# A decoder layer's input projection: 22 column blocks taken in pairs, ahead of the head groups, and the scan's y products two chunks at a time

## The chip, the core and the metric

The kernel runs on one core of a Trainium2 chip. The metric is device time in microseconds of one execution. A core has a matrix engine (TensorE, PE in the profile; its weight loads are shown as PEld), a vector engine (VectorE, DVE), a scalar engine (ScalarE, ACT), GpSimd (POOL), and SyncE (SP), which issues nearly all DMAs of this kernel.

## What is computed

One step of a hybrid decoder layer on 1024 prompt tokens and 8 decode tokens, T = 1032 token columns in all, model width 1024.

```python
xn = rms_norm(x, p['norm_mix_pre'])
z, xbc, dt_raw, u_pool, gate_a, gate_b = split(xn @ p['w_in'])   # 2048 | 4096 | 32 | 1024 | 1024 | 1024
xbc_c = silu(causal_conv(xbc, conv_w, conv_b))                    # x (2048), B (8 x 128), C (8 x 128)
y = ssd_scan(xs, dt, a, B, C, h0) + d_skip * xs                   # 8 groups of 4 heads, chunks of 128 tokens
y_a = rms_norm(y * silu(z), ssm_norm)
y_b = pool_mix(u_pool, ...)                                       # trailing means of 2/4/8/16, grouped product
merged = sigmoid(gate_a) * (y_a @ w_branch_a) + sigmoid(gate_b) * (y_b @ w_branch_b)
h = x + rms_norm(merged @ w_out)
out = h + rms_norm((silu(g) * up) @ w_ffn_out)                    # g, up = rms_norm(h) @ w_ffn_in
```

## The kernel before

Everything is held transposed: 128 features on the partitions, the 1032 tokens along the free dimension. A product in fp32 precision is made of three matmuls of a shorter type (`mm3`, L230 to L232): the weights are split in a high and a low part (`wh`, `wl`, made by a copy on ACT, L166, and a subtraction, L167), the activations too (`xh`, `xl`), and high·high, high·low and low·high are summed in PSUM.

The input projection's columns come in blocks of 128: 16 of z (`WZ`), 16 of x, 8 of B, 8 of C, 8 of the pooling input (`WU`), 8 and 8 of the two gates (`WGA`, `WGB`). A block takes three units (`in_unit`), one for each third of the tokens (344 columns); a unit is 8 feature rows times 3 matmuls, 24 matmuls into one PSUM bank of the tag `pj`, which has 4 banks. The other four banks are `T` (2), `S` (1) and `y` (1).

The order of the stages:

1. Norm, the time steps dt and the pooling branch: per pooling group two blocks are projected (`pool_proj`), averaged on DVE (`pool_group`), split, and multiplied by a small matrix (`pool_mix`). The last group's product is made inside the first head group.
2. Head groups 0 to 7. `group_proj(g)` makes the six blocks of group g (B, C, x0, x1, z0, z1: 18 units). Each of the first four is followed by a convolution: ACT L593, three DVE instructions L595, ACT L596, DVE L597. Each z unit ends in a tanh on ACT (L610) and a DVE instruction (L611). `ssd(g-1)`, the scan of the group before, is interleaved, one step of it after each unit (`interleave(..., 1)`). A scan has 18 steps: in an even step `stage1(c)` of chunk c, in an odd one `stage2` of the chunk three steps earlier, and decode work on some.
3. `gates`: the 16 gate blocks, with `ssd(7)` interleaved, one step after each unit; the gates are stored in memory (`s_ga`, `s_gb`).
4. Branch products (`quarters`, six of them), merge, output projection, norms, FFN and final norm. FFN in (around L1094) already uses seven products of 258 columns where the plain form has eight.

In a scan, `stage1(c)` transposes B and x of the chunk into a `T` bank (L667 to L670), makes `xdt`, `wx` and `CB` on DVE (L675, L677, L679), loads the decay rows into a tile `E` of three buffers by DMA (L681), and turns them into the chunk's 128x512 decay matrix (ACT L683, L685, DVE L686). `stage2(c)` makes the state update and the old state's part in the `S` bank (L703, L705), then eight matmuls of 64 columns of the array into the `y` bank (L709): two chunks share that one bank, half each, and after the odd chunk DVE reads it (L724). DVE also reads `S` (L716, L719), POOL scales the state (L715) and adds to Y (L728).

The program is written in this order, and a scheduler lays out each engine's queue from it before the run: the order in the text is a priority, and an instruction that the scheduler holds to be ready may go ahead of an earlier one that it holds not to be. On the chip each queue is then worked off strictly in order, the queue of SP's DMAs too. Row buffers (`row`, 36 of them with 128x1032 or a little more) are shared by nearly everything.

Of the kernel before, what the change touches and what calls it, by code (L numbers as in the profile page):

```python
# [16 lines left out]
P = 128  # L17
# [6 lines left out]
G = 8  # L24
# [29 lines left out]

PP_G1, PP_GPOST, PP_GFFN, PP_GFPOST = 0, 8, 16, 24
# [16 lines left out]
def interleave(main, side, every):  # L72
    n = 0
    for _ in main:
        n += 1
        if side is not None and n % every == 0:
            if next(side, StopIteration) is StopIteration:
                side = None
    if side is not None:
        for _ in side:  # L80
            pass
# [3 lines left out]
def layer_kernel(ctx: ExitStack, tc: tile.TileContext, xT, wi, wdt, wpool, wba, wbb, wo, wfi,  # L85
# [9 lines left out]
    ps = ctx.enter_context(tc.tile_pool(name="ps", bufs=2, space=PSUM))  # L95
# [3 lines left out]

    def bank(tag):  # L100
        return ps.tile([P, 512], F32, name=tag, tag=tag, bufs={"pj": 4, "T": 2, "S": 1, "y": 1}[tag])

# [1 line left out]
    plan = []  # L104

# [3 lines left out]
    def plan_weights():  # L109
        def u_blocks(gi):  # L110
            for kb in range(2):
                want(("in", WU + 2 * gi + kb), wi[WU + 2 * gi + kb], eng=pool if 2 * gi + kb == 1 else dve)
        u_blocks(0)
        for gi in range(3):
            u_blocks(gi + 1)
            want(("pool", gi), wpool[gi], 512)
        for g in range(G):
            for i, blk in enumerate((WB + g, WC + g, WX + 2 * g, WX + 2 * g + 1, WZ + 2 * g, WZ + 2 * g + 1)):
                want(("in", blk), wi[blk])
                if g == 0 and i == 2:  # L120
                    want(("pool", 3), wpool[3], 512)
        for base in (WGA, WGB):
            for ob in range(KT):
                want(("in", base + ob), wi[base + ob])
        for qi in range(6):
            for obp in range(4):
                want(("br", qi, obp), wba[qi, obp] if qi < 4 else wbb[qi - 4, obp], eng=pool if qi == 0 else dve)
# [16 lines left out]
    def w_dma():  # L144
        i = stage["nd"]
        if i < len(plan):
            _, src, n, _, _, kind = plan[i]
            if kind == "big":
                raw = big(n, "wu")
            else:  # L150
# [40 lines left out]
    x_rows = [row(name="xrow") for _ in range(KT)]  # L191
# [36 lines left out]

    def mm3(out, wh, wl, xh, xl, start, stop):
        pe.matmul(out, wh, xh, start=start, stop=False)  # L230
        pe.matmul(out, wh, xl, start=False, stop=False)  # L231
        return pe.matmul(out, wl, xh, start=False, stop=stop)  # L232

# [131 lines left out]
    def pool_group(gi, us):  # L365
        w = 2 << gi
        ds = []
        for kb in range(2):
# [12 lines left out]
            while st < w:  # L381
# [6 lines left out]
                st *= 2  # L388
            ss = const.tile([P, NS], F32, name="ss", tag="ss", bufs=2)
# [7 lines left out]
            ds.append(d)  # L397
        return ds
# [12 lines left out]
    def pool_mix(gi, dh, dl):  # L411
        wh, wl = load_w("pool", gi)
        for ob in range(2):
            blk = 2 * gi + ob
            yb = row(name="yb")
            for th in range(3):
                pt = bank("pj")
# [109 lines left out]

    dt_setup()
    us = pool_proj(0, True)
    pend = pool_split(pool_group(0, us))  # L530
    an = dt_phase(dt_mm(2))
    us = pool_proj(1)
    pool_mix(0, *pend)
    pend = pool_split(pool_group(1, us))
    dt_phase2(an)
    us = pool_proj(2)
    pool_mix(1, *pend)
    pend = pool_split(pool_group(2, us))
    us = pool_proj(3)
    pool_mix(2, *pend)  # L540
    last_mix = pool_group(3, us)

# [1 line left out]
    s_y = dram.tile([16, P, T], F32, name="s_y")  # L544
    s_ga = dram.tile([KT, P, T], F32, name="s_ga")
    s_gb = dram.tile([KT, P, T], F32, name="s_gb")
# [17 lines left out]
    def conv_proj(g):  # L564
# [4 lines left out]
        for j, (key, blk, cb) in enumerate((("B", WB + g, 16 + g), ("C", WC + g, 24 + g),  # L569
# [4 lines left out]
            us = U[:, SOFF:SOFF + 32].rearrange("p (b k) -> p b k", k=4)  # L574
# [14 lines left out]

            def tap(k):  # L590
                i = 32 + cb * 4 + k
                return hcw[:, i:i + 1]
            act.activation(out=S[:, :CW], in_=U[:, 0:CW], func=AF.Identity, scale=tap(0), bias=hcw[:, cb:cb + 1])  # L593
            for k in range(1, 4):
                dve.scalar_tensor_tensor(out=S[:, :CW], in0=U[:, k:k + CW], scalar=tap(k), in1=S[:, :CW], op0=ALU.mult, op1=ALU.add)  # L595
            act.activation(out=U[:, 0:CW], in_=S[:, :CW], func=AF.Tanh)  # L596
            dve.scalar_tensor_tensor(out=S[:, :CW], in0=U[:, 0:CW], scalar=1.0, in1=S[:, :CW], op0=ALU.add, op1=ALU.mult)  # L597
# [4 lines left out]
    def z_proj(g):  # L602
        d = grp[g]
        for j in range(2):
            wt = load_in(WZ + 2 * g + j)
            Z = row(name="Z")
            d[f"z{j}"] = Z
            for th in range(3):
                pt = in_unit(wt, th)
                act.activation(out=Z[:, TH[th]], in_=pt, func=AF.Tanh, scale=0.5)  # L610
                dve.scalar_tensor_tensor(out=Z[:, TH[th]], in0=Z[:, TH[th]], scalar=1.0, in1=pt,  # L611
                                         op0=ALU.add, op1=ALU.mult)
                yield
# [4 lines left out]

    def gates():
        n = 0  # L620
        for base, dst in ((WGA, s_ga), (WGB, s_gb)):
            for ob in range(KT):
# [686 lines left out]
```

## Time and profile before

| | |
|---|---|
| Median of three runs | 2149.07 us (2146.68 to 2152.36) |
| Profiled execution, span | 2146.5 us, 2.6 us under the median |
| PE busy | 2091.0 us, 97% of the span |
| PEld busy | 2055.9 us, 96% |
| DVE busy | 1361.0 us, 63% |
| ACT busy | 791.1 us, 37% |
| POOL busy | 406.9 us, 19% |
| Memory traffic | 243.74 MB, 114 GB/s |
| Pooling branch, norm and dt | 0 to about 145 us |
| Group 0's blocks, no scan beside them | about 145 to 222 us |
| Seven groups with a scan beside them | about 222 to 833 us |
| Gates with the last scan | about 833 to 1032 us |
| Branch products | about 1032 to 1306 us |
| Output projection, norms, FFN | the rest |

Matmuls are pipelined, so their shown durations overlap; what one costs in a full stream is the length of the stretch divided by their number. The times at which stages change were read from the first and last start of each line's instructions.

### The profile page before, as it was taken

To read this page: it belongs to the slowest core of one execution; us is meant where nothing else is said; L and a number is where in the kernel's file an instruction comes from. 1 tells how busy PE (TensorE), PEld (TensorE's weight loads), DVE (VectorE), ACT (ScalarE), POOL (GpSimd) and SP (SyncE) were. 2 spreads that over 40 slices of the span, in tenths; PEclk is the share of its full clock that TensorE was granted. 3 is DMA by queue.
4 is the path that set the end of the run, shared out by engine and by line. 5 is a ranking of instruction groups with operands and counts; after the bars stand their busy time and mean duration, and the time that the engine had idled before them with its cause. 6 is when DMAs were issued, how large, how long until landed. Compare 5 with 4: busy or idle time off the path is not lost.

```text
span 2146.5 us, 36509 instructions
## 1 busy us (share of the span) xinstructions
PE 2091.0 (97%) x14722; PEld 2055.9 (96%) x14722; DVE 1361.0 (63%) x2283; ACT 791.1 (37%) x1530; POOL 406.9 (19%) x407
## 2 busy tenths in 40 slices
PE   6999999999999999999999999989999999999997
PEld 5999999999999999999999999989999999999997
DVE  7665578677787776422155775679777666654436
ACT  5443344444444444233331024445333233351112
POOL 3100234424434243210100001352000000000004
PEclk9999999999999999999999999989999999999998
DMA  3332343334434334433343444234322222252133
GB/s 126 97 112 72 100 125 125 124 105 142 139 99 127 116 128 149 137 118 136 117 150 101 145 135 151 101 101 142 96 95 90 72 78 90 99 188 69 40 101 107
DMA packets 121961, 243.74 MB, mean 114 GB/s; under 512 B 24896, under 2 KB 62912, under 8 KB 121792
## 3 DMA queue, kind: packets, MB, share of 16 engines
q1 hardware_dynamic: 121360, 241.12, 35.0%
q8 instruction: 116, 1.90, 0.4%
q14 instruction: 53, 0.43, 0.1%
q10 hardware_dynamic: 432, 0.28, 0.0%
HBM read 189.38 MB, written 51.98 MB: 112 GB/s over the span
## 4 chain that ended last, share of the span: by engine, by line
PE 71%; DVE 8%; ACT 2%; DMA 2%; issue 2%; POOL 2%; SPq 0%; DVEq 0%; ACTq 0%; POOLq 0%
PE pj L230 20%; PE pj L232 20%; PE pj L231 20%; DVE S L595 2%; DMA E<-s_ac 1%; PE y L709 1%; PE y L230 1%; PE y L231 1%; PE y L232 1%; DVE S L597 1%; PE T L230 1%; PE T L232 1%; PE T L231 1%; PE S L231 1%; PE S L232 1%
## 5 line engine op out<-in xcount | busy, mean ns | idle before, releaser
L230 PE MATMUL pj<-xh,wh 128*128 128x344 f32 x1728 | 563.3, 327 | 2.4 <-ACT xh L299 2.4
L231 PE MATMUL pj<-xl,wh 128*128 128x344 f32 x1728 | 553.0, 320 | 0.1
L232 PE MATMUL pj<-xh,wl 128*128 128x344 f32 x1728 | 552.8, 320 | 0.0
L230 PEld LDWEIGHTS pj<-xh,wh 128*128 128x128 f32 x1728 | 324.9, 188 | 14.3 <-issue 11.0
L231 PEld LDWEIGHTS pj<-xl,wh 128*128 128x128 f32 x1728 | 325.5, 188 | 1.4 <-DVE xl L300 0.8
L232 PEld LDWEIGHTS pj<-xh,wl 128*128 128x128 f32 x1728 | 325.2, 188 | 0.0
L167 DVE TENSOR_TENSOR wl<-wr,wh 128x1024 fp32r<-128x1024 f32 (+1 forms) x125 | 170.4, 1364 | 210.0 <-ACT wh L166 210.0
L166 ACT CAST wh<-wr 128x1024 fp32r<-128x1024 f32 x142 | 146.6, 1033 | 363.4 <-PE pj L231 335.5
L917 POOL TENSOR_TENSOR ssacc<-ssacc,sq 128x258 f32<-128x258 f32 (+3 forms) x41 | 43.7, 1072 | 923.8 <-ACT sq L916 917.7
L230 PE MATMUL pj<-qh,wh 128*128 128x344 f32 (+1 forms) x608 | 189.7, 312 | 0.0
L231 PE MATMUL pj<-ql,wh 128*128 128x344 f32 (+1 forms) x608 | 189.7, 312 | 0.0
L232 PE MATMUL pj<-qh,wl 128*128 128x344 f32 (+1 forms) x608 | 189.6, 312 | 0.0
L231 PE MATMUL pj<-al,wh 128*128 128x344 f32 (+2 forms) x528 | 168.9, 320 | 0.0
L232 PE MATMUL pj<-ah,wl 128*128 128x344 f32 (+2 forms) x528 | 168.8, 320 | 0.0
L230 PE MATMUL pj<-ah,wh 128*128 128x344 f32 (+2 forms) x528 | 168.8, 320 | 0.0
L683 ACT ACTIVATE E<-E,acT 128x128 f32<-128x128 f32 x256 | 83.9, 393 | 214.8 <-DMA E<-s_ac 198.1
L595 DVE SCALAR_TENSOR_TENSOR S<-U,hcw,S 128x1056 f32<-128x1056 f32 x96 | 137.3, 1430 | 3.0 <-ACT S L593 2.9
L1172 DVE TENSOR_TENSOR acc<-acc,pj 128x344 f32<-128x344 f32 (+2 forms) x120 | 60.8, 510 | 98.0 <-PE pj L232 97.9
L231 PEld LDWEIGHTS pj<-ql,wh 128*128 128x128 f32 x608 | 114.4, 188 | 0.0
L232 PEld LDWEIGHTS pj<-qh,wl 128*128 128x128 f32 x608 | 114.4, 188 | 0.0
L230 PEld LDWEIGHTS pj<-qh,wh 128*128 128x128 f32 x608 | 114.3, 188 | 0.0
L232 PEld LDWEIGHTS pj<-ah,wl 128*128 128x128 f32 x528 | 99.3, 188 | 0.0
(351 smaller groups left out, 4898.1 us busy)
## 6 DMA issues: line engine op xcount, KB each, us to landing
wr<-wi SPq DMA_DIRECT2D x72, 512.0 KB, 4.3
E<-s_ac SPq DMA_DIRECT2D x64, 256.0 KB, 4.0
wr<-wfi SPq DMA_DIRECT2D x30, 512.0 KB, 3.6
s_act<-wk SPq DMA_DIRECT2D x44, 258.0 KB, 2.0
ar<-s_act SPq DMA_DIRECT2D x22, 516.0 KB, 4.7
wu<-wfi SPq DMA_DIRECT2D x22, 512.0 KB, 3.7
wr<-wfo SPq DMA_DIRECT2D x20, 512.0 KB, 3.7
s_y<-Y SPq DMA_DIRECT2D x16, 516.0 KB, 3.8
```

The lines of the kernel that those rows point to most:

```text
L166: act.copy(out=wh, in_=raw)
L167: eng.tensor_tensor(out=wl, in0=raw, in1=wh, op=ALU.subtract)
L230: pe.matmul(out, wh, xh, start=start, stop=False)
L231: pe.matmul(out, wh, xl, start=False, stop=False)
L232: return pe.matmul(out, wl, xh, start=False, stop=stop)
L595: dve.scalar_tensor_tensor(out=S[:, :CW], in0=U[:, k:k + CW], scalar=tap(k), in1=S[:, :CW], op0=ALU.mult, op1=ALU.add)
L597: dve.scalar_tensor_tensor(out=S[:, :CW], in0=U[:, 0:CW], scalar=1.0, in1=S[:, :CW], op0=ALU.add, op1=ALU.mult)
L683: act.activation(out=E[:, h], in_=E[:, h], func=AF.Relu, scale=-1.0, bias=acT[:, c, 4 * g + h:4 * g + h + 1])
L709: pe.matmul(o, xdt[:, h, :], E[:, h, :], start=True, stop=True)
L917: eng.tensor_tensor(out=sacc[:, sl], in0=sacc[:, sl], in1=q, op=ALU.add)
L1172: dve.tensor_tensor(out=acc[ob][:, sl], in0=acc[ob][:, sl], in1=pt, op=ALU.add)
```

## The change

The core of the diff. What is left out are the tile pools that it opens and closes around the stages (`xp`, `ps1` with three two-bank tiles `dj`, `ps2` with `pj` 3, `T` 2, `S` 1, `y` 2 banks, `ps3` as before), renames, and the same conv code moved into a helper.

```diff
+H = T // 2
+PAIRS = "ga0 ga1 z0 ga2 z1 ga3 gb0 z2 gb1 z3 gb2".split()
+MIXES = {2: 3}
+RING = 3
+PROD1 = ("B11", "T2", "B21", "T3", "T1", "T4", "B22")
...
+    def pair_blocks(name):
...
+        if kind == "z":
+            return WZ + 4 * n + 1, WZ + 4 * n + 3
+        base = (WGA if kind == "ga" else WGB) + 2 * n
+        return base, base + 1
...
+    def t_sums():
+        for k in range(4):
+            a, b, c, d = (x_rows[i][:, sl] for i in (k, 4 + k) for sl in (lo_, hi_))
+            eng.tensor_tensor(out=d, in0=d, in1=b, op=ALU.subtract)
+            eng.tensor_tensor(out=b, in0=b, in1=a, op=ALU.subtract)
+            eng.tensor_tensor(out=a, in0=a, in1=d, op=ALU.add)
+            eng.tensor_tensor(out=c, in0=c, in1=a, op=ALU.subtract)
...
+    def t1_split():
+        for k in range(4):
+            for i, r_ in enumerate((xh[k], xl[k])):
+                sync.dma_start(out=s_b12[i, k], in_=r_[:, hi_].bitcast(F32))
+        for k in range(4):
+            act.copy(out=xh[k][:, hi_], in_=x_rows[k][:, hi_])
+            dve.tensor_tensor(out=xl[k][:, hi_], in0=x_rows[k][:, hi_], in1=xh[k][:, hi_], op=ALU.subtract)
+
+    def restore():
+        for k in range(4):
+            for i, r_ in enumerate((xh[k], xl[k])):
+                sync.dma_start(out=r_[:, hi_].bitcast(F32), in_=s_b12[i, k])
...
+    def prep1(i):
...
+            dve.tensor_tensor(out=s_[:, a_], in0=u_[:, a_], in1=u_[:, b_], op=ALU.add)
+            dve.tensor_tensor(out=s_[:, b_], in0=s_[:, a_], in1=g_[:, a_], op=ALU.subtract)
...
+            dve.tensor_tensor(out=u_[:, a_], in0=g_[:, a_], in1=u_[:, a_], op=ALU.subtract)
...
+            dve.tensor_tensor(out=s_[:, b_], in0=g_[:, b_], in1=s_[:, b_], op=ALU.subtract)
...
+        act.copy(out=w[:, a_], in_=src)
+        dve.tensor_tensor(out=w[:, b_], in0=src, in1=w[:, a_], op=ALU.subtract)
...
+    def product1(i):
...
+        if pi in (0, 1, 3, 4):
+            pair[pi] = dbank()
+        pt = pair[{2: 0, 5: 3, 6: 4}.get(pi, pi)]
...
+        for b_ in range(2):
+            cs = slice(b_ * Q, b_ * Q + Q)
+            o = pt[:, b_ * 512:b_ * 512 + Q]
+            for k in range(4):
...
+                pe.matmul(o, wh_, h[:, cs], start=first and k == 0, stop=False, skip_group_check=True)
+                pe.matmul(o, wh_, l[:, cs], start=False, stop=False, skip_group_check=True)
+                pe.matmul(o, wl_, h[:, cs], start=False, stop=k == 3, skip_group_check=True)
...
+        if pi == 0:
+            act.copy(out=q22, in_=v)
+        elif pi == 1:
+            dve.tensor_tensor(out=q12, in0=q22, in1=v, op=ALU.add)
+        elif pi == 2:
+            act.copy(out=q11, in_=v)
...
+    def finish_pair(name, rs):
...
+        if kind == "z":
+            for j in (1, 0):
+                t = row(name="tz")
+                act.activation(out=t, in_=rs[j], func=AF.Tanh, scale=0.5)
+                dve.scalar_tensor_tensor(out=rs[j], in0=t, scalar=1.0, in1=rs[j], op0=ALU.add, op1=ALU.mult)
+                sync.dma_start(out=s_z[2 * n + j], in_=rs[j])
...
-    last_mix = pool_group(3, us)
+    with tc.issue_after(fence):
+        t_sums()
+    pool_mix(2, *pend1)
+    for i in range(RING):
+        prep1(i)
+    t_split()
...
+    for i, (name, pi) in enumerate(items1):
+        if i + RING < len(items1):
+            prep1(i + RING)
+        product1(i)
...
+        if name != "m" and pi == 6:
+            tails.append(finish_pair(name, pair["rows"]))
...
+    BANKS[0] = {"pj": 3, "T": 2, "S": 1, "y": 2}
+    restore()
...
         def stage2(c, BT, xdt, wx, eA, E):
-            if c % 2 == 0:
-                pend[1] = bank("y")
-            yb = pend[1]
...
-            for h in range(R):
-                o = yv[(h % 2) * 64:(h % 2) * 64 + 64, h // 2, c % 2, :]
-                pe.matmul(o, xdt[:, h, :], E[:, h, :], start=True, stop=True)
+            if c % 2 == 0:
+                pend[0] = xdt, E
+            else:
+                yb = bank("y")
+                for i, (x_, E_) in enumerate((pend[0], (xdt, E))):
+                    for h in range(R):
+                        o = yv[(h % 2) * 64:(h % 2) * 64 + 64, h // 2, i, :]
+                        pe.matmul(o, x_[:, h, :], E_[:, h, :], start=True, stop=True)
...
+            if u == 13:
+                d["z1"] = row(name="Z")
+                sync.dma_start(out=d["z1"], in_=s_z[g])
...
-        interleave(group_proj(g), ssd(g - 1), 1)
-    interleave(gates(), ssd(G - 1), 1)
+        interleave(group_proj(g), ssd(g - 1), 1.17)
+    interleave(gates(), ssd(G - 1), 1.1)
```

After the change:

- Eleven pairs of blocks (four of gate A, three of gate B, and four of z, each the second z block of two groups) are made between the pooling branch and group 0. A pair is a 1024 x 256 weight block times 1032 tokens, cut in two in each dimension; seven products of the halves (sums and differences of weights in `prep1`, of activations in `t_sums` and `t_split`) stand for eight. A product is 2 x 4 x 3 matmuls of 258 columns into a tile of two banks; its result is added to the pair's rows on DVE or copied by ACT. Gates and z then get their tanh and are stored in memory.
- The activation sums T1 take the place of half of four `xh` and `xl` rows, which are stored in memory first (`s_b12`) and loaded again at the end (`restore`).
- The last pooling group's work (`last_pool`) and its product (`m`) lie among the first pairs.
- `group_proj` makes five blocks (15 units); z1 is loaded from memory in the scan's step 13. About 1.17 scan steps go with a unit.
- The scan makes the y products of an even and an odd chunk together, in the odd one's `stage2`, into one of two `y` banks; `xdt` has three buffers, `CB` one. `pj` has three banks in this stage.
- `gates` has only gate B's last two blocks (6 units), then the first branch quarter (24 units of 12 matmuls), with `ssd(7)` at 1.1 steps per unit. The row norm of the scan (`ssm_rms`) moves into the third quarter.

## Rows read from the trace of the kernel before

**Rows 1.** Page, part 1: busy time, share of span and instructions of each engine.

```profile
PE 2091.0 (97%) x14722; PEld 2055.9 (96%) x14722; DVE 1361.0 (63%) x2283; ACT 791.1 (37%) x1530; POOL 406.9 (19%) x407
```

**Rows 2.** Windows: stretch, length, busy us (count) of PE PEld DVE ACT POOL, PEclk, DMA, GB/s.

```profile
200.00:250.00 50.00, 50.00 (x332) 49.03 (x331) 25.63 (x33) 16.20 (x31) 9.93 (x9) 1.00 0.28 94
...
1000.00:1100.00 100.00, 100.00 (x636) 100.00 (x635) 29.38 (x31) 38.31 (x57) 9.61 (x4) 1.00 0.42 148
...
1500.00:1854.00 354.00, 354.00 (x2949) 354.00 (x2950) 256.29 (x496) 118.70 (x242) 0.00 (x0) 1.00 0.27 86
```

**Rows 3.** Instructions of L654, the first of each scan: durations, first and last start.

```profile
L654 PE MATMUL T<-ident,bcs x8: 271/271/272, 221.7 to 833.6; 128*16 128x128 f32 x8
```

**Rows 4.** Waits of all engines: who waited for whom, us, times, longest us.

```profile
PE y L709 <- DVE Y L724: 12.2, 9, 1.6
PE pj L230 <- ACT mo L943: 2.6, 1, 2.6
...
ACT E L683 <- DMA E<-s_ac: 198.1, 39, 9.4
```

**Rows 5.** Timeline of PE, one `stage2` and next scan's start: start, length, merged instructions.

```profile
567.21 0.61 PE L705 MATMUL S<-S,hT 128*128 128x128 f32 x4
567.74 0.66 PE L709 MATMUL y<-E,xdt 128*64 128x128 f32 x8
568.33 0.43 PE L230 MATMUL pj<-xh,wh 128*128 128x344 f32 x1
568.60 0.32 PE L231 MATMUL pj<-xl,wh 128*128 128x344 f32 x1
...
572.21 0.27 PE L654 MATMUL T<-ident,bcs 128*16 128x128 f32 x1
572.32 0.27 PE L667 MATMUL T<-ident,S 128*128 128x128 f32 x1
```

**Rows 6.** Groups by line and form, whole span: count, busy us, mean ns, idle before.

```profile
L1110 DVE TENSOR_TENSOR wk<-wk,pj 128x258 f32<-128x258 f32 x120 | 50.5, 422 | 21.3 <-PE pj L232 20.4
L1129 DVE TENSOR_TENSOR wk<-wk 128x516 f32<-128x516 f32 x40 | 27.8, 696 | 1.7
```

**Rows 7.** Windows of one group's period, columns as in Rows 2.

```profile
514.20:602.00 87.80, 85.63 (x583) 82.20 (x582) 66.64 (x95) 40.81 (x91) 34.25 (x36) 1.00 0.39 124
```

**Rows 8.** DVE's groups by line and form in 539 to 627 us, one group's period.

```profile
L595 DVE SCALAR_TENSOR_TENSOR S<-U,hcw,S 128x1056 f32<-128x1056 f32 x12 | 17.6, 1466 | 0.0
L167 DVE TENSOR_TENSOR wl<-wr,wh 128x1024 fp32r<-128x1024 f32 x6 | 9.6, 1607 | 8.2 <-ACT wh L166 8.2
L686 DVE TENSOR_TENSOR E<-E,CB 128x512 f32<-128x512 f32 x8 | 6.6, 823 | 0.1
L597 DVE SCALAR_TENSOR_TENSOR S<-U,S 128x1056 f32<-128x1056 f32 x4 | 6.2, 1543 | 2.2 <-ACT U L596 2.2
...
L750 DVE TENSOR_TENSOR st<-st,dts 128x1024 f32<-128x1024 f32 x3 | 3.6, 1210 | 0.0
...
L611 DVE SCALAR_TENSOR_TENSOR Z<-Z,pj 128x344 f32<-128x344 f32 x6 | 3.0, 506 | 7.4 <-ACT Z L610 7.4
...
L778 DVE TENSOR_TENSOR Y<-Y,Z 128x1032 f32<-128x1032 f32 x2 | 2.9, 1482 | 0.5 <-POOL Y L728 0.5
...
L754 DVE TENSOR_TENSOR st<-st,bc 128x1024 f32<-128x1024 f32 x1 | 1.2, 1210 | 0.0
```

**Rows 9.** Timeline of DVE and POOL: a weight split beside decode work; x1's last conv step.

```profile
542.67 2.40 POOL L756 TENSOR_TENSOR bc<-st,bc 128x1024 f32<-128x1024 f32 x1 [2.99 <-DVE dx L747]
...
543.26 2.90 DVE L167 TENSOR_TENSOR wl<-wr,wh 128x1024 fp32r<-128x1024 f32 x1
...
553.94 1.26 DVE L597 SCALAR_TENSOR_TENSOR S<-U,S 128x1056 f32<-128x1056 f32 x1 [0.84 <-ACT U L596]
```

**Rows 10.** Tile `qr`, 516 KB loads: time from issue to landing.

```profile
DMA to landing us min/median/max: 4.5/5.6/8.2
```

**Rows 11.** Window at a stall of PE before FFN in, columns as in Rows 2.

```profile
1410.00:1414.00 4.00, 1.27 (x4) 0.97 (x5) 1.28 (x3) 0.81 (x3) 4.00 (x2) 0.50 0.00 0
```

More of the change, by code (lines that the diff above doesn't have):

```diff
@@ L69, in schedule, with interleave @@
         pass
[L72 to L76, printed above, removed]
+def interleave(main, side, steps):
+    for n, _ in enumerate(main):
+        for _ in range(int((n + 1) * steps) - int(n * steps) if side is not None else 0):
             if next(side, StopIteration) is StopIteration:
                 side = None
+                break
     if side is not None:
@@ L188, in load_raw @@
         return raw
-    x_rows = [row(name="xrow") for _ in range(KT)]
+    x_rows = [xp.tile([P, T], F32, name="xrow", tag="x") if k < 4 else row(name="xrow") for k in range(KT)]
     def load_x(th):
@@ L539, in layer_kernel, with last_pool @@
+    fence = last_mm[0].ins
     us = pool_proj(3)
-    pool_mix(2, *pend)
-    last_mix = pool_group(3, us)
+    with tc.issue_after(fence):
+        t_sums()
+    pool_mix(2, *pend1)
+    del pend1
+    for i in range(RING):
+        prep1(i)
+    t_split()
+    x_rows.clear()
+    pend = []
+    ps_ctx.close()
+    ps_ctx = ExitStack()
+    ps[0] = ps_ctx.enter_context(tc.tile_pool(name="ps1", bufs=2, space=PSUM))
+    tails = []
+    def last_pool(us_):
+        ds_ = []
+        yield from pool_steps(3, us_, ds_)
+        dh, dl = [], []
+        for d in ds_:
+            dh.append(row(dt=F32R, name="dh"))
+            act.copy(out=dh[-1], in_=d[:, :T])
+            dl.append(row(dt=F32R, name="dl"))
+            dve.tensor_tensor(out=dl[-1], in0=d[:, :T], in1=dh[-1], op=ALU.subtract)
+            yield
+        pend.append((3, (dh, dl)))
@@ L588, in conv_proj @@
             d[key] = S
[L590 to L597, printed above, removed]
+            conv(U, S, cb)
             if j == 3:
@@ L603, in z_proj @@
         d = grp[g]
[L604 to L613, printed above, removed]
+        wt = load_in(WZ + 2 * g)
+        Z = row(name="Z")
+        d["z0"] = Z
+        for th in range(3):
+            pt = in_unit(wt, th)
+            act.activation(out=Z[:, TH[th]], in_=pt, func=AF.Tanh, scale=0.5)
+            dve.scalar_tensor_tensor(out=Z[:, TH[th]], in0=Z[:, TH[th]], scalar=1.0, in1=pt,
+                                     op0=ALU.add, op1=ALU.mult)
+            yield
     def group_proj(g):
```

303 lines of the change are left out of this document (232 added, 71 removed).

## The prediction

> **What bounds the kernel now.** I read the page's busy times first: PE 97%, its weight loads 96%, DVE 63% [rows 1]. So only what shortens PE's stream, or the few places where PE stands, can pay. Busy time does not price a matmul, since durations overlap; the windows do. Where nothing but 344-column matmuls runs, 636 fit in 100 us: 157.2 ns each. Where nothing but 258-column ones runs (FFN in, itself seven products for eight), 2949 fit in 354 us: 120.0 ns, with DVE busy 72% of that stretch [rows 2]. The second view is the waits: after the start and the norms, PE's largest repeated wait is the y products' for DVE's read of their single bank, 12.2 us in 9 waits [rows 4]. The third is the period of a head group, from the first instruction of each scan: (833.6 - 221.7) / 7 = 87.4 us [rows 3]. In such a period DVE is busy 66.6 us and POOL 34.3 us [rows 7]: far busier than over the whole span, so a shorter period is where a second bound could show.
>
> **Part 1, the pairs.** Removed: 22 blocks of 72 matmuls, so per pair 144 x 157.2 ns = 22.64 us. Added: 7 products of 24 matmuls at 120.0 ns = 20.16 us [rows 2]. Gain 2.48 us a pair, **27.2 us** for eleven. By columns alone it would be an eighth of 22.64, 2.83 us a pair; the narrower matmul carries more overhead, so I take the measured prices. The new DVE work is hidden: per pair 4 weight sums, 7 splits at about 0.70 us (512 columns; the 516-column row is 696 ns), 5 additions from PSUM at 0.70 to 0.84 us (two of 258 columns are 2 x 422 ns [rows 6]; I take 0.75), 11.5 us, and 3 us more for z (two of 1.5): 12 to 15 us in 20, no denser than FFN in's 72%. Two products into the same two-bank tile need the first to be read out in between, but another product of 24 x 0.12 = 2.9 us lies there. If that cover failed, it would cost up to the whole 2.48 us a pair (a rival below).
>
> **Part 2, y products.** The 12.2 us wait arises because the next even chunk reuses the bank before DVE has read it [rows 4]. With two banks the read in question is two chunks older, about 10 us; it is gone, **12.2 us**. What is next late at that place is DVE's read of the `S` bank, needed a chunk later. Merging also drops every other run of 64-column matmuls. Around one such run [rows 5]: the four L705 before it take 0.53 us until it starts, where 128-column matmuls go 0.11 us apart (4 x 0.11 = 0.44), and the first projection matmul after it takes 0.27 instead of 0.157. So entry and exit cost 0.09 + 0.11 = 0.20 us. 32 runs are dropped: at most 6.4 us, nothing if the S products pay the same on leaving. I take **5 us**, since both excesses are seen at this run alone. Sum of gains: 27.2 + 12.2 + 5 = 44.4 us.
>
> **Part 3, three changes of PSUM layout.** New banks wait for the old ones' last reads. The trace has no such change. From below it is 0.4 us (one read, 422 ns [rows 6]), from above a wait of PE for a read by ACT, 2.6 us [rows 4]. I take 1.2 us, nearer to the plain read, each: **3.6 us** (1 to 8).
>
> **Part 4, start of the pairs.** `t_sums` is 16 DVE instructions at 0.70 = 11 us in the last pooling projection, where DVE is about half idle (25.6 of 50 us [rows 2]): hidden. `t_split`, 16 splits, 11 us, falls partly on the first pair, beside 11.5 us of the pair's own work and `last_pool`. T4 is due after five products, 14.4 us; before it lie 12 splits, 8.4 us (t43 and T1), 5.6 us of weight preparation and 3 us of additions: 17 us. Some can be done earlier, but 36 row buffers are nearly all held then (16 `xh`/`xl`, 4 x rows, 12 for T, 4 of the previous mix), so not all. Bounds 0 (done early) and 7 us (the last splits after 14.4 us, with a product's wait); I take **2 us**, the shortfall.
>
> **Part 5, end of the pairs.** `restore` issues 8 loads of 264 KB after the last pair's T1 product. Four loads of 516 KB, the same bytes, land within 8.2 us [rows 10]. Until the first unit's second third needs them, two products and a third of a block run: 5.8 + 3.8 = 9.5 us. So it is just hidden. If SP's queue holds them behind the last pair's store, which waits for an addition and a tanh after the last product, they start some 8 us later and cost about 6.7 us. Bounds 0 and 6.7, I take **2 us**. The other new DMAs (`s_b12` out, `s_z` out and in, 12 MB in 244) find DMA engines under half busy [rows 2, 7].
>
> **Part 6, groups.** A period loses one block (72 x 157.2 ns = 11.3 us), the y wait (1.4 us) and four runs (0.6): 87.4 - 13.3 = 74.1 us on PE. DVE loses three z instructions (1.5 us) and one weight split (1.6) [rows 8]: 63.5 us, 86% of it. All I claim here is counted in parts 1 and 2; the question is what DVE gives back. The tightest place is x1's convolution: its last step ends at 555.2, and the next scan's first transpose comes at 572.2 [rows 5, 9], 17 us of slack. Three units (11.3 us) and about two scan steps' PE work (2.4) leave it: 3 us. In the units before, two more scan steps fall (1.17 per unit), each 1.7 us of DVE work (66.6 less convolutions 23.8, splits 9.6 and z 3.0, over 18 steps [rows 7, 8]). So the slack is about used up. Bounds 0 and 24 us (those 3.4 us in each of seven groups, no slack left); I take **8 us**, about one a group, nearer to nothing because the scheduler can put ready projections first. Three `pj` banks hold three units, 11.3 us; the longest time ACT was held up by the decay load is 9.4 us [rows 4], so the fourth bank is not missed.
>
> **Part 7, last scan.** Its later steps go beside branch units of 12 matmuls (1.89 us). A chunk takes two steps and, of PE, (87.4 - 67.9 - 1.4) / 8 = 2.3 us, so it now has 2 x 1.89 / 1.1 + 2.3 = 5.7 us where it had 2 x 3.77 + 2.3 = 9.8. DVE's work for it is 2 x 1.7 = 3.4 us, plus weight and quarter splits: near 5. Bounds 0 and 8 us; I take **3 us**, since 14 branch units remain to fill gaps.
>
> Sum: -44.4 + 3.6 + 2 + 2 + 8 + 3 = -25.8; the profiled span of 2146.5 becomes 2120.7. The profile's span lies 2.6 us under the median, so **2123 us**.
>
> **Rivals.**
>
> *DVE and POOL bound the groups (slower).* For it: a weight split took 2.90 us, against 1.21 for a decode instruction of the same size, and it ended just after the POOL instruction that it met [rows 8, 9]. If the DVE lines that read two tensors from SBUF and all of POOL exclude each other, one period needs 17.6 + 8.0 + 6.6 + 6.2 + 3.6 + 2.9 + 2.4 us on DVE (split less one block; L754 twice) [rows 8] and 34.3 on POOL [rows 7]: 81.6 us, 7.5 over 74.1, 52.5 us in seven groups. Without part 6's 8 us the sum is -33.8, so the kernel ends at 2146.5 - 33.8 + 52.5 + 2.6 = 2168 us. It turns slower above 74.1 + 33.8 / 7 = 78.9 us a period. Against it: these durations contain the waits, so 81.6 counts some time twice. The Trainium skill, page "SBUF — State Buffer", section "Who interferes with whom", says just this: VectorE's second read port is GpSimd's, and the pair is an exclusive lock, so the loser stands for the other's whole instruction. The trace agrees in the one meeting shown, a split that lasted until POOL was done.
>
> *The y wait moves rather than goes:* DVE is just as late, and the `S` bank or the decay matrix is waited for instead. Then 17.2 us are not won: 2140 us. Against it: nothing on PE waited for those in the trace.
>
> *Each pair waits for its read-outs or operands* by the 2.5 us that it saves: 27.2 us lost, 2150 us, no change. Against it: the seven-product stage of FFN in streams without loss [rows 2].
>
> *Nearly nothing is given back:* costs of 5 us, 2110 us.
>
> A real stall costs more than itself: beside the 2.6 us wait ahead of FFN in [rows 4], PE was busy 1.27 us of four and the granted clock was 0.50, the 1.2 GHz level [rows 11]. That is why the range reaches past the central costs.
>
> **How the numbers follow.** Chances: the forecast (2113 to 2136) 0.65; y wait moved (2140) 0.10; little given back (2106 to 2112) 0.09; pairs wait (2150) 0.07; DVE and POOL bound (2168) 0.09. The range 2106 to 2145 leaves the last two out, about 0.16; with no cost at all, and 6.4 us instead of 5 for the runs, the time would be 2103, so the low end lies just above. A measurement here can tell 0.3%, 6.4 us: the limits are 2142.6 and 2155.5. Faster: 0.65 + 0.09 + most of 0.10 = 0.83. Same: 0.08. Slower: 0.09.
>
> **What would show it.** Seven products of a pair in 20.2 us, 168 matmuls at 120 ns, DVE at 60 to 75% there; no wait of the y products for DVE's read of their bank; L654 (its line moves) at a period of 74 to 76 us; short stands of PE at the three bank changes. I am wrong if the period is near 80 us, if PE waits for decay matrices or convolution outputs in each group, or if the pairs take over 22 us each.

## The result, and the profile after

The changed kernel takes **2122.03 us** (median of four runs, 2118.37 to 2125.4); the kernel before took 2147.88 us beside it. The ratio is 0.9872, with a 95% interval of 0.9853 to 0.9890. The profiled execution has a span of 2120.3 us, against 2146.5. The forecast was 2123 (2106 to 2145): the time is right. Some of its parts are not, and the experiments show one that is wrong by far more than the total lets one see. Line numbers below are those of the changed kernel or of the run that is named; edits that take lines out shift them a little.

The page's busy times, the line that answers to [rows 1]:

```profile
PE 2058.1 (97%) x14986; PEld 2027.5 (96%) x14986; DVE 1467.2 (69%) x2455; ACT 824.1 (39%) x1573; POOL 398.9 (19%) x405
...
PE 81%; DVE 10%; ACT 3%; DMA 3%; issue 2%; POOL 1%; SPq 0%; DVEq 0%; POOLq 0%; ACTq 0%
```

The last line is the split by engine of the chain that ended last. DVE has 106 us more work, and PE is still the engine that sets the time. Two windows, with the columns of [rows 2]: the pairs, and one period of a head group (which answers to [rows 7]):

```profile
146.96:376.70 229.74, 228.20 (x1884) 227.59 (x1884) 144.52 (x210) 93.75 (x145) 0.31 (x2) 1.00 0.34 112
588.50:663.30 74.80, 73.39 (x512) 70.88 (x511) 62.89 (x91) 38.39 (x85) 33.65 (x35) 1.00 0.45 145
```

The first instruction of each scan, as in [rows 3] (its line is now L893), gives the period: (961.9 - 438.3) / 7 = 74.8 us, where it was 87.4.

```profile
L893 PE MATMUL T<-ident,bcs x8: 270/270/272, 438.3 to 961.9; 128*16 128x128 f32 x8
```

PE's waits, as in [rows 4], those that this change made or moved, and ACT's wait for the decay load:

```profile
PE S L938 <- ACT wh L194: 6.9, 7, 1.0
...
PE S L938 <- DVE eA L961: 4.1, 8, 1.0
...
PE pj L261 <- DVE ql L1058: 2.7, 1, 2.7
...
PE dj L700 <- ACT gt L705: 1.5, 1, 1.5
PE T L527 <- DVE dta L525: 1.4, 1, 1.4
...
ACT E L922 <- DMA E<-s_ac: 114.5, 32, 7.4
```

The 12.2 us of the y products are gone. In their place PE waits 11.0 us, in 15 waits, at the state products `S`. Seven of these are put down to ACT's weight copy, but the timeline of one shows who was late (DVE, ACT and PE, merged instructions):

```profile
506.19 1.04 ACT L194 CAST wh<-wr 128x1024 fp32r<-128x1024 f32 x1 [0.49 <-PE pj L261]
506.41 0.41 DVE L958 TENSOR_TENSOR hT<-hT,S 128x256 f32<-128x256 f32 x1
506.74 0.41 DVE L961 TENSOR_TENSOR eA<-eA,S 128x256 f32<-128x256 f32 x1
...
507.30 0.67 PE L938 MATMUL S<-wx,BT 128*128 128x256 f32 x2 [1.00 <-ACT wh L194]
```

DVE's read of the single `S` bank ends at 507.15, the product starts 0.15 us later; the weight copy, which it doesn't use, merely ended at about the same time. With a second `S` bank (s_two_banks, below) all 15 are gone, so they are for that bank's reader.

Where the time went, from the starts of the stages' first PE instructions in both traces (negative is won):

| part | forecast, us | measured, us | from what |
|---|---|---|---|
| 1, pairs | -27.2 | -26.5 | 22 x 11.32 = 249.0 of blocks gone, 229.7 - 5.7 (pooling product) - 1.5 (the stall of part 4) = 222.5 in their place |
| 3, PSUM layout changes | +3.6 | +3.4 | 0.8, 1.0 and 1.5, over the usual spacing |
| 4, start of the pairs | +2 | +1.5 | wait `dj` for `gt` L705 |
| 5, end of the pairs | +2 | 0 | no stand of PE before group 0's first units |
| 2 and 6, seven groups | -9.2 | -9.0 | 7 x (87.41 - 74.80 - 11.32) |
| 7, last scan and first branch units | +3 | +3.5 | three stands, 2.9, 1.2 and 0.7 over the usual spacing, less four dropped runs, 1.3 |
| not foreseen | 0 | +1.9 and -1.1 | pooling branch; behind the branch products |
| sum | -25.8 | -26.3 | the spans differ by 26.2 |

### The profile page after: what moved, and what is told of

Read it like the earlier page. It is cut to its first block, busy times and chain, and to the rows that moved or that the text cites. A ratio compares the mean times of both kernels' runs of the same rounds, so it can differ in the third digit from the quotient of the medians.

```text
span 2120.3 us, 37445 instructions
## 1 busy us (share of the span) xinstructions
PE 2058.1 (97%) x14986; PEld 2027.5 (96%) x14986; DVE 1467.2 (69%) x2455; ACT 824.1 (39%) x1573; POOL 398.9 (19%) x405
## 4 chain that ended last, share of the span: by engine, by line
PE 81%; DVE 10%; ACT 3%; DMA 3%; issue 2%; POOL 1%; SPq 0%; DVEq 0%; POOLq 0%; ACTq 0%
PE pj L260 19%; PE pj L261 19%; PE pj L262 19%; PE dj L702 3%; PE dj L700 3%; PE dj L701 3%; DVE S L725 2%; DMA E<-s_ac 2%; DVE wl L195 1%; PE y L950 1%; PE S L938 1%; ACT wh L194 1%; PE y L260 1%; PE y L261 1%; PE y L262 1%
## 5 line engine op out<-in xcount | busy, mean ns | idle before, releaser
L260 PE MATMUL pj<-xh,wh 128*128 128x344 f32 x1200 | 392.1, 329 | 3.2 <-ACT xh L330 2.4
L261 PE MATMUL pj<-xl,wh 128*128 128x344 f32 x1200 | 385.3, 321 | 0.1
L262 PE MATMUL pj<-xh,wl 128*128 128x344 f32 x1200 | 384.0, 320 | 0.0
L194 ACT CAST wh<-wr 128x1024 fp32r<-128x1024 f32 (+1 forms) x119 | 123.4, 1037 | 363.8 <-PE pj L261 330.9
L260 PEld LDWEIGHTS pj<-xh,wh 128*128 128x128 f32 x1200 | 226.0, 189 | 8.2 <-issue 4.7
L261 PEld LDWEIGHTS pj<-xl,wh 128*128 128x128 f32 x1200 | 226.5, 189 | 1.7 <-DVE xl L331 0.8
L262 PEld LDWEIGHTS pj<-xh,wl 128*128 128x128 f32 x1200 | 226.5, 189 | 0.0
L195 DVE TENSOR_TENSOR wl<-wr,wh 128x1024 fp32r<-128x1024 f32 (+1 forms) x104 | 140.4, 1351 | 115.1 <-ACT wh L194 104.6
L261 PEld LDWEIGHTS pj<-al,wh 128*128 128x128 f32 x528 | 99.2, 188 | 0.0
```

What stands on the lines that cost most here:

```text
L194: act.copy(out=wh, in_=raw)
L195: eng.tensor_tensor(out=wl, in0=raw, in1=wh, op=ALU.subtract)
L262: last_mm[0] = pe.matmul(out, wl, xh, start=False, stop=stop)
```

## Experiments

All ratios are to the kernel before on the same chip; times are medians. "Period" is that of a head group, read from L893 as above.

**Is the merging needed?** The first run (y_split_runs) undid the merging of the y products alone and kept both banks.

```diff
-            if c % 2 == 0:
-                pend[0] = xdt, E
-            else:
-                yb = bank("y")
...
+            if c % 2 == 0:
+                pend[1] = bank("y")
+            yb = pend[1]
...
+            for h in range(R):
+                o = yv[(h % 2) * 64:(h % 2) * 64 + 64, h // 2, c % 2, :]
+                pe.matmul(o, xdt[:, h, :], E[:, h, :], start=True, stop=True)
```

> The changed kernel with the y products of each chunk made in its own stage2 again, as before, into half of a bank, but with the two y banks and three pj banks kept. Theory A (dropping a run of 64-column matmuls is worth what the two traces now show, (87.4 - 1.66) - (74.8 - 1.85) - 11.32 = 1.47 us a group, 0.37 us a run): 32 runs more cost 11.8 us, 2134 us, and the group's period rises by 1.5 us to 76.3. Rival (the forecast's 0.15 us a run): 5 us, 2127 us, period 75.4.

Measured: **2179.62 us**, ratio 1.0151 (1.0132 to 1.0169), period 82.6. Neither theory came near. Undoing this one part costs 57.6 us and makes the kernel slower than before. PE's waits, and one period in a window:

```profile
PE S L938 <- DVE eA L958: 46.6, 21, 5.3
...
604.30:686.40 82.10, 75.95 (x509) 71.95 (x508) 62.25 (x90) 38.24 (x83) 33.44 (x36) 0.98 0.41 132
```

DVE does the same work in a period as in the changed kernel (62.3 us against 62.9), so it is not saturated; it is late. (The expectation of split_runs_s_two, below, puts the waits at `S` at 73 us; the view shows these 46.6.) Taken by the kind of neighbouring PE instructions, the seven periods are 54.4 us longer: 36 us are stands of over 0.48 us at the `S` products, 14 us the entries and exits of the 28 runs that are back, and 6 us projection matmuls at 164 instead of 161 ns, at a granted clock of 0.98 over these seven periods instead of 1.00 (more on it below). The timeline of DVE ahead of one of these stands, and PE's instruction that ends it:

```profile
660.88 0.41 DVE L958 TENSOR_TENSOR eA<-eA,S 128x256 f32<-128x256 f32 x1
661.21 1.52 DVE L993 TENSOR_TENSOR st<-st,bc 128x1024 f32<-128x1024 f32 x1
...
665.24 1.22 DVE L999 TENSOR_REDUCE ys<-bc 128x8 f32<-128x1024 f32 x1 [2.44 <-POOL bc L995]
...
666.64 1.22 DVE L195 TENSOR_TENSOR wl<-wr,wh 128x1024 fp32r<-128x1024 f32 x1
...
669.87 1.31 DVE L725 SCALAR_TENSOR_TENSOR S<-U,hcw,S 128x1056 f32<-128x1056 f32 x1
671.09 0.69 DVE L925 TENSOR_TENSOR E<-E,CB 128x512 f32<-128x512 f32 x1
671.70 1.31 DVE L725 SCALAR_TENSOR_TENSOR S<-U,hcw,S 128x1056 f32<-128x1056 f32 x1
672.92 0.42 DVE L955 TENSOR_TENSOR hT<-hT,S 128x256 f32<-128x256 f32 x1
673.25 0.42 DVE L958 TENSOR_TENSOR eA<-eA,S 128x256 f32<-128x256 f32 x1
...
673.82 0.67 PE L938 MATMUL S<-wx,BT 128*128 128x256 f32 x2 [2.36 <-DVE eA L958]
```

`S` was filled at 661.4 to 662.5 and its last read starts at 673.25: between lie a wait of 2.44 us for POOL's decode product, a weight split, a convolution and the next decay matrix, all ahead of the reader in DVE's queue. PE's next `S` product is due, finds its only bank unread and stands. Four more runs asked what holds this unmerged scan. First (pairs_old_y), besides the unmerged products, one y bank and four `pj` banks as before:

```diff
-    BANKS[0] = {"pj": 3, "T": 2, "S": 1, "y": 2}
+    BANKS[0] = {"pj": 4, "T": 2, "S": 1, "y": 1}
```

> Part 1 without part 2: the eleven pairs are made as in the changed kernel, but the scan makes its y products chunk by chunk as before, into one y bank, with four pj banks. By the terms of the prediction (12.2 us of wait and 5 us of runs not won) it takes 2123 + 17 = 2140 us. By what y_split_runs showed (groups of five blocks need the merged runs) it takes 2175 us or more, slower than before, and the period of a group is 82 us or more: then the pairs' gain of 25 us is lost wherever the scan is not merged, and the change's two halves are not a sum. Rival to that: the period is near 87.4 - 11.3 = 76.1 us.

Measured: 2176.92 us, 1.0128 (1.0113 to 1.0143), period 82.7. The prediction's terms would give 2140; they are wrong here by 37 us. Then the unmerged scan with a second `S` bank and one of y (split_runs_s_two):

```diff
-    BANKS[0] = {"pj": 3, "T": 2, "S": 1, "y": 2}
+    BANKS[0] = {"pj": 3, "T": 2, "S": 2, "y": 1}
```

> y_split_runs (chunk by chunk, 2179.6 us, 73 us of waits of the S products for DVE's eA read) with two S banks and one y bank. Theory A (the single S bank, read late, is what holds PE): those waits fall below 20 us, the old wait of y for its bank (12 us) comes back, and the time is about 2179.6 - 50 + 12 = 2142 us (2130 to 2150). Theory B (the scan's own chain is late: DVE makes the next state too late, whatever the banks): the wait moves to the state hT, 50 us or more stay, and the time stays above 2165 us.

Measured: 2180.02 us, 1.0141 (1.0126 to 1.0156), period 82.6. The wait for the bank does go, and PE waits nearly as long, 41.4 us for 46.6, for the next two things, the bank of y and the state itself:

```profile
PE y L948 <- DVE Y L963: 22.5, 10, 3.2
PE S L940 <- DVE hT L955: 18.9, 7, 3.3
```

So the bank is where PE is seen to stand, not what holds it. Then, again with two y banks as in the first run, one scan step per unit instead of 1.17 (split_runs_even):

```diff
-        interleave(group_proj(g), ssd(g - 1), 1.17)
+        interleave(group_proj(g), ssd(g - 1), 1)
```

> y_split_runs with one scan step per unit, as before the change, in place of 1.17; the last three steps of each scan then lie behind the last unit of the group. Theory A (too many scan steps per unit of projection make DVE late): the waits in the covered part fall to what before had, under 10 us in all, the uncovered three steps cost up to 3 us a group, and the time is about 2179.6 - 60 + 20 = 2140 us. Theory B (the separate runs are the cause at any pitch): the time stays at 2170 us or above, and S waits for DVE's eA read stay the largest of the repeated waits.

Measured: 2178.71 us, 1.0125 (1.0102 to 1.0148), period 82.1. The covered steps run almost without a stand, but the last steps of each scan, behind the group's last unit, hold PE 5.1 us in every group: the loss changes its place, not its size. Last (pairs_old_scan), pairs_old_y with the scan's SBUF buffers as before too, so the pairs beside the scan's old code, at 1.17 steps a unit:

```diff
-        bcr = sp.tile([P, P], F32, name="bcr", tag="BT")[:16]
+        bcr = sp.tile([16, P], F32, name="bcr", tag="bcr", bufs=1)
...
-            xdt = sp.tile([P, R, 64], F32, name="xdt", tag="xdt", bufs=3)
+            xdt = sp.tile([P, R, 64], F32, name="xdt", tag="xdt")
...
-            CB = sp.tile([P, P], F32, name="CB", tag="CB", bufs=1)
+            CB = sp.tile([P, P], F32, name="CB", tag="CB")
```

> Part 1 without any of part 2: pairs_old_y (2176.9 us, a period of 82.7 us) with the scan's SBUF buffers also as before: two xdt, two CB, and bcr in a buffer of its own. The changed kernel pays for its third xdt with the second CB and with bcr, which then lives in one of BT's two buffers until its store has landed; the runs so far that undid the merging kept these. Theory A (the buffers given away are what holds the unmerged scan: in y_split_runs ACT's BT copies wait 12.1 us for that store, and DVE's xdt 45.3 us for those copies, against 10.4 us in the changed kernel): those two waits fall to about nothing and 10 us, the period goes to about 76 to 78 us, and the time is near the 2140 us that the sum of the prediction's parts gives (2135 to 2150). Theory B (five blocks of projection per group are too little cover for a scan that needs each decay matrix and each state chunk by chunk, whatever its buffers): the period stays above 81 us and the time above 2168 us.

Measured: **2171.63 us**, 1.0106 (1.0077 to 1.0134), period 81.5. ACT's wait for the store of `bcr` is gone, and DVE's wait for `BT` is 39.8 us, where 10 were expected: the buffers given away cost some 5 us (the two intervals overlap), not 37.

```profile
L893 PE MATMUL T<-ident,bcs x8: 272/272/272, 438.1 to 1008.6; 128*16 128x128 f32 x8
```

What follows: **the pairs with the scan's old code make the kernel 1.1% slower.** In five runs, which changed y banks, `S` banks, pitch and buffers in turn, the unmerged scan's period stayed at 81.5 to 82.7 us. That it can't go lower is not shown: the old buffers were not combined with the old pitch. What the merging brings without the pairs has no measurement: with its third `xdt`, and `bcr` in a buffer of its own, the scan's buffers need 19.94 kB of a partition, and 19.59 are left beside the old row buffers. With six blocks in a group (87.4 us) no such loss showed.

Why the merged scan can go lower is only partly settled. Counted from the starts of PE's instructions in groups 1 to 6, this many projection matmuls lie between a chunk's first transpose and its first y product (chunks 0 to 7):

```
before        72  72  72  72  72  72  72  72
after        120  72  96  72  96  48  72  48
y_split_runs  72  72  48  72  72  48  48  48
```

From transposes to y the quickest chunk took 11.0 us on average in the changed kernel, while 48 matmuls cover 7.5 us and 72 cover 11.3. Unmerged, at 1.17 steps a unit, four of eight chunks have 7.5 us; merged, two have, and each of these stands beside one with 72 to 96. No run changed this cover and left the runs as they were, so that it is the cause is not shown.

Where PE stands speaks for something narrower. In pairs_old_scan 33.4 of the 34.6 us that PE waits at `S` and y in the seven groups lie at one place of each scan, chunk 2. Here is the third scan, PE and DVE:

```profile
621.47 0.61 PE L940 MATMUL S<-S,hT 128*128 128x128 f32 x4
...
625.09 0.68 DVE L925 TENSOR_TENSOR E<-E,CB 128x512 f32<-128x512 f32 x1
628.04 1.22 DVE L999 TENSOR_REDUCE ys<-tmp 128x8 f32<-128x1024 f32 x1 [2.27 <-POOL tmp L995]
629.18 0.41 DVE L955 TENSOR_TENSOR hT<-hT,S 128x256 f32<-128x256 f32 x1
629.51 0.42 DVE L958 TENSOR_TENSOR eA<-eA,S 128x256 f32<-128x256 f32 x1
630.07 0.67 PE L938 MATMUL S<-wx,BT 128*128 128x256 f32 x2 [2.93 <-DVE eA L958]
...
632.94 0.47 DVE L963 SCALAR_TENSOR_TENSOR Y<-S,ppt,y 128x256 f32<-128x256 f32 x1
633.55 1.12 PE L948 MATMUL y<-E,xdt 128*64 128x128 f32 x8 [2.37 <-DVE Y L963]
```

Chunk 1 filled `S` at 622.1, and DVE has read it 7.8 us later. Ahead of the reader in its queue is the decode work's reduction, which waits 2.27 us for POOL and itself delays the reader by 1.1; an estimate from these lines: without them the read ends at 626.5, and PE begins to wait at 627.1. The read of y comes later still, between two steps of a convolution. In the changed kernel the reduction comes behind the reader, which is done 3.2 us after `S` was filled (610.3 in the run of PE's instructions shown further down):

```profile
613.10 0.41 DVE L961 TENSOR_TENSOR eA<-eA,S 128x256 f32<-128x256 f32 x1
```

In both kernels the `S` products of these two chunks lie 24 projection matmuls apart (48 before the change), so at this place the cover is the same and DVE's order differs. Before the change the reduction was ahead of the reader too (`S` read after 5.9 to 6.7 us), and 48 matmuls covered it. Moving that one instruction in the unmerged scan was not tried; it is an open rival to the view that this scan needs the merged runs.

**Which banks does the merged scan need?** First one y bank, and the eighth bank left empty (y_one_bank):

```diff
-    BANKS[0] = {"pj": 3, "T": 2, "S": 1, "y": 2}
+    BANKS[0] = {"pj": 3, "T": 2, "S": 1, "y": 1}
```

> The changed kernel with one y bank instead of two (the eighth bank left unused). Theory A: merged, the bank is written every second chunk and read by DVE within some 3 us, so one bank does and PE waits for S as before: 2122 us, no wait of the y products. Rival (the second bank is what took the 12.2 us wait away): the wait for DVE's read of y returns, 10 to 12 us, 2133 us.

Measured: 2117.93 us, 0.9855 (0.9837 to 0.9874), period 74.7, no wait of y. The second y bank, on which the prediction put its 12.2 us, is worth nothing: once two chunks' products are made together, the bank is written at once and has two chunks' time to be read. Then the eighth bank given to `S` (s_two_banks):

```diff
-    BANKS[0] = {"pj": 3, "T": 2, "S": 1, "y": 2}
+    BANKS[0] = {"pj": 3, "T": 2, "S": 2, "y": 1}
```

> The changed kernel with the second bank given to S instead of y (S 2, y 1). Theory A (PE's 13 us of short waits at the state products are for DVE's late read of the one S bank): they go, the group's period falls by up to 1.8 us to 73, 2109 to 2113 us. Rival (DVE is late altogether, and the wait moves on to the next thing that DVE frees or to y): period 74.5 to 75, 2120 to 2124 us, with another wait of 1 to 2 us a group shown.

Measured: 2114.17 us, 0.9838 (0.9817 to 0.9859), period 73.7. The waits for the bank's reader are gone, half of their time comes back as a wait for the state:

```profile
PE S L940 <- DVE hT L958: 5.5, 7, 1.0
```

In 74.8 us PE thus has 1.1 us that a bank holds (74.8 - 73.7) and 0.8 that the scan's own chain holds (5.5 / 7).

**What the last three pairs bring.** Gate B's blocks 0 to 5 as plain blocks again, eight pairs (gate_b_plain; the later loading of the first branch quarter is left out of the cut):

```diff
-PAIRS = "ga0 ga1 z0 ga2 z1 ga3 gb0 z2 gb1 z3 gb2".split()
+PAIRS = "ga0 ga1 z0 ga2 z1 ga3 z2 z3".split()
...
-        for ob in (6, 7):
+        for ob in range(KT):
```

> The changed kernel with gate B's three pairs taken back: gate B's eight blocks are made in the plain form beside the last scan, and the first branch quarter's splits come 18 units later. Theory A (a pair saves 22.64 us against 20.4 us as measured, 2.3 us): 6.8 us more, less the 4.7 us of waits of PE beside the last scan, which the plain units cover again: 2124 to 2127 us. Rival (the pairs won little, the time came from elsewhere): 2122 us or less.

Measured: 2121.1 us, 0.9872 (0.9857 to 0.9887): no difference, where three pairs at 2.4 us should cost 7.2. With 18 units more beside the last scan, from that scan's first instruction to the output projection it takes 380.7 us; less those units (18 x 3.77 = 67.9) that is 312.8, where the changed kernel takes 318.8. So 6.0 us come back there. Three of the eleven pairs only pay for taking the last scan's cover away.

**The stand at the first branch units.** PE stands 2.7 us for `ql` at 991.75, and DVE and POOL show this beside it:

```profile
987.28 3.32 POOL L195 TENSOR_TENSOR wl<-wr,wh 128x1024 fp32r<-128x1024 f32 x1
...
988.32 4.93 DVE L1058 SCALAR_TENSOR_TENSOR ql<-qr,ppt,qh 128x1032 fp32r<-128x1032 f32 x2
...
991.75 0.42 PE L261 MATMUL pj<-ql,wh 128*128 128x344 f32 x1 [2.67 <-DVE ql L1058]
```

The first of the two `ql` takes 3.37 us, where their median is 1.29, and ends 1.1 us after POOL's instruction does. Loading this operand one unit earlier and splitting it two units earlier (split_early):

```diff
-                if n == 2:
+                if n == 1:
                     load_quarter(0)
-                elif n >= 5:
-                    split_quarter(0, n - 5)
+                elif n >= 3:
+                    split_quarter(0, n - 3)
...
-        for j in (2, 3):
-            split_quarter(0, j)
```

> The changed kernel with the first branch quarter's rows loaded after the first instead of the second of the six gate units, and split after units 3 to 6 instead of 5, 6, 6 and 6. Theory A (the 2.7 us wait of PE at 991 us is for a split that DVE did late): it goes, 2119 us. Rival (row buffers are all held there, so that the loads can't come earlier): nothing moves, 2122 us.

Measured: 2118.6 us, 0.9860 (0.9845 to 0.9874). The wait is gone from the trace, but another stands in its place, at the one `S` bank of the last scan, again behind a decode reduction that waits for POOL:

```profile
992.93 1.22 DVE L1002 TENSOR_REDUCE ys<-tmp 128x8 f32<-128x1024 f32 x1 [2.83 <-POOL tmp L998]
...
994.40 0.41 DVE L961 TENSOR_TENSOR eA<-eA,S 128x256 f32<-128x256 f32 x1
994.96 0.67 PE L938 MATMUL S<-wx,BT 128*128 128x256 f32 x2 [2.06 <-DVE eA L961]
```

From the last scan's start to the output projection this run takes 318.5 us, the changed kernel 318.8: the edit wins nothing there. The 3.4 us between the medians come from stretches that it doesn't touch, and the two intervals overlap.

**DVE's load, and the shared port.** One of the five weight splits of a group on POOL instead of DVE (c_split_pool):

```diff
-                want(("in", blk), wi[blk])
+                want(("in", blk), wi[blk], eng=pool if blk == WC + g else dve)
```

> The changed kernel with one of the five weight splits of each group moved from DVE to POOL. DVE loses 1.2 to 1.6 us of 62.9 a period, POOL gains 2.7 us. Theory of the shared port (an instruction of either that reads two tensors from SBUF waits for the other's whole length): the sum of both grows, DVE's other instructions get longer, PE's waits at S stay or grow, 2122 to 2128 us. Rival (DVE's own queue alone makes PE wait): the waits shrink by a few us, 2116 to 2121 us.

Measured: 2120.01 us, 0.9865 (0.9845 to 0.9884), period 74.65: no difference.

```profile
586.90:661.50 74.60, 73.25 (x511) 70.74 (x510) 63.26 (x90) 38.31 (x85) 34.63 (x36) 1.00 0.45 145
```

DVE has an instruction less and is busy 63.3 us instead of 62.9. Over the whole kernel its weight splits take 9.8 us less (128.5 for 138.3), and its decay-matrix products (L925) 8.3 us more, 936 ns each instead of 806: what it no longer does, it loses in another line that reads two tensors.

**The order of dt and pooling.** The changed text starts the dt product ahead of the first pooling group; undone (dt_order):

```diff
-    cp = dt_mm(2)
     pend1 = pool_split(pool_group(0, us))
-    an = dt_phase(cp)
+    an = dt_phase(dt_mm(2))
```

> The changed kernel with the pooling branch's dt product back behind the first group's averaging and split, as before. Theory A (the 1.9 us by which the pooling branch grew, 1.4 of it a wait for DVE's dta at 96.8 us, come from that move): the wait goes and the first product of the pairs starts at 145 us instead of 147.0; 2120 us. Rival (DVE is later there for another reason, the weight split's place or the x sums): no change, 2122 us.

Measured: 2120.96 us, 0.9868 (0.9852 to 0.9883), and the wait of L527 for `dta`, 1.4 us, is still there; the pairs start at 147.7, not earlier. That theory falls, and where the 1.9 us of the pooling branch come from stays open.

**Both edits together,** two `S` banks and the earlier split (s_two_split_early):

> The two edits that each gave a little are made together: two banks for the S products with one for y, and the first branch quarter loaded and split earlier. Theory (independent terms): s_two_banks ended 7.9 us below the changed kernel and split_early 3.4 us, at different places (groups, and the start of the branch units), so the sum is about 2111 us (2107 to 2114). Rival (the same slack is used twice: with two S banks the last scan is already off PE's path): 2114 us, as s_two_banks alone.

Measured: **2108.27 us** (2107.03 to 2109.23), 0.9808 (0.9793 to 0.9822), better than both kernels. Of the 15 us between the two profiled spans (2120.3 and 2105.3), 7.8 lie in the groups (period 73.7), 3.7 between the last scan's start and the output projection, and 3.5 behind it, where neither edit touches anything; that last stretch lies between 836.1 and 841.7 us in the runs here, whatever the edit. The total is the one that independent terms forecast, but the terms are not independent: from the last scan's start to the output projection two `S` banks alone win 0.9 us, the earlier split alone 0.3, both 3.7, since with the second bank the stand that replaced the wait for `ql` is gone too.

## Why the prediction was right, and where it was not

**Part 1** held: 20.4 us a pair (224.0 / 11; 20.2 without the stall at the start) for 20.16, with matmuls 120 ns apart, and DVE busy 63% of that stretch where 60 to 75% was expected. Its start cost 1.5 us, not by late splits but by a late read-out: the third product waited for ACT, whose copy of the first result was queued behind the eight casts of `t43h`. **Parts 3 and 4** came within 0.5 us. **Part 5** was priced at 2 and cost nothing: the loads of `restore` were hidden, as the working said before the reserve for SP's queue was added.

**Parts 2 and 6** are right as a sum (-9.2 and -9.0) and wrong inside. The wait of y did go, and 11.0 of the 12.2 us came back at `S`, one place further on: the rival "the y wait moves rather than goes" was right about the mechanism, and the sentence that named DVE's read of `S` as next late should have been a term of the sum. Part 6's 8 us "given back" are this wait; its place, x1's convolution with 3 us of slack, was not where PE stood. That the sum still meets the measured one is luck: 11 us less was won on the wait, about 5 more on the runs, and 8 had been set against them. What the rival lacked is the size of the merged runs. The forecast took 0.15 us for each; the trace of after shows about 0.32. A run at 610.22 and, 5 us on, a chunk without one:

```profile
609.68 0.61 PE L940 MATMUL S<-S,hT 128*128 128x128 f32 x4
610.22 1.10 PE L950 MATMUL y<-E,xdt 128*64 128x128 f32 x16
611.24 0.33 PE L906 MATMUL T<-ident,S 128*128 128x128 f32 x1
...
616.04 0.61 PE L940 MATMUL S<-S,hT 128*128 128x128 f32 x4
616.40 0.41 PE L260 MATMUL pj<-xh,wh 128*128 128x344 f32 x1
```

Over all groups, the last `S` product is followed by a y product after 205 ns and by a projection after 31 ns, and a y product by a projection after 202 ns and by another y product after 55: a run dropped is 205 + 202 - 31 - 55 = 321 ns, 10.3 us for 32 runs where 5 were taken. The prediction priced the leaving of a run by the first projection matmul's 0.27 us against 0.157. But that matmul takes 243 ns behind an `S` product too, and 263 behind a run, so next to nothing of that excess is the run's; its price is the step into that matmul, 202 ns against 31. The Trainium skill, page "TensorEngine Tiling (Array Packing)", section "Key Properties", says that a change of tiling mode drains the engine; the 205 and 202 ns beside 31 agree.

**What the sum hid.** Part 1 booked the z block taken out of each group at PE's full price, 11.3 us, and part 2 as 17.2 us beside it. The two are not separate terms. With the scan's old code, a group loses 5.9 of those 11.3 us (87.4 - 81.5), and without part 2 the kernel is slower than before, not 2140. The step that failed is "a period loses one block" on PE, with DVE's busy time (63.5 of 74.1) and the slack of x1's convolution as the only other bounds: it asked whether DVE has time enough, and not whether each read of `S` and y still comes in time with the scan's steps closer together. In pairs_old_scan it doesn't: at chunk 2 PE stands for both reads, 4.8 us a group (33.4 / 7). The time came out right because part 2 was there.

**Part 7** was 3 and is 3.5; the stand for `ql` is most of it. The rival **DVE and POOL bound the groups** did not come (74.8 us a period against 78.9), but its mechanism is there: the `ql` above and c_split_pool, where a load moved from DVE to POOL did not shorten DVE's busy time. The rule of the Trainium skill weighed there (page "SBUF — State Buffer", section "Who interferes with whom") fits both: the twelve `ql` that meet no POOL instruction take 1.28 to 1.30 us. In the weight split of [rows 9], "just after the POOL instruction" is 1.1 us after it, about the length of an undisturbed one. That **each pair waits** (2150) or that **nearly nothing is given back** (2110) did not come: a pair took 20.4 us, and PE has 11 us of new waits in the scans.

## What to carry to other kernels

When work is taken away beside an interleaved chain, ask for each step of the chain whether what is left beside it covers the answer: here PE's busy 97% let the groups look free to shrink, and the old scan kept 5.4 of every 11.3 us. Of a wait on a single buffer, ask who is late and what is queued ahead of him; a second buffer moves the wait to the next thing that the same engine delivers, as s_two_banks and split_runs_s_two show, and an operand that comes earlier can do the same (split_early). And parts that make one thing possible together have no prices of their own: undo each by itself before saying what it brings.

## What was not expected of the hardware

A stand of PE can cost more behind it. In y_split_runs the 2.4 us stand that ends at 673.82 (window 669.4 to 673.8, PE busy 2.06 of 4.4 us) is followed by 4.2 us at a granted clock of 0.59, so mostly at the 1.2 GHz level: some 1.7 us more.

```profile
669.40:673.80 4.40, 2.06 (x14) 1.79 (x13) 4.40 (x8) 1.08 (x2) 0.31 (x1) 1.00 0.41 160
673.80:678.00 4.20, 4.18 (x20) 3.60 (x21) 4.20 (x9) 2.26 (x6) 2.73 (x3) 0.59 0.02 4
```

It does not always: in the changed kernel PE is busy 1.33 of the 4 us from 988 to 992, and the granted clock stays at 1.00 there and in the next 4 us.

```profile
988.00:992.00 4.00, 1.33 (x9) 1.05 (x8) 4.00 (x3) 0.15 (x1) 4.00 (x2) 1.00 0.21 16
992.00:996.00 4.00, 3.96 (x26) 3.63 (x25) 2.78 (x6) 0.45 (x2) 4.00 (x4) 1.00 0.88 308
```

What decides between the two is not shown here.
